# A norm cut into feature blocks and token columns, with three products fed in step

## The chip, the cores and the metric

The kernel runs on one core of one Trainium2 chip. The metric is the device time of one execution in microseconds, the median of several runs. Engines are named as the profile names them: PE (TensorE, with PEld for its weight loads), DVE (VectorE), ACT (ScalarE), POOL (GpSimd), SP (the queue that issues most reads).

## What is computed: the reference

Two layers over 512 latent and 256 context tokens of 1024 features:

```python
for l in range(DEPTH):                                   # 2
    mod_x = split(silu(c) @ ada_w[l] + ada_b[l], 6)      # shift, scale, gate of the mixer; the same of the MLP
    mod_c = split(silu(c_ctx) @ ada_w[l] + ada_b[l], 6)
    hx = rmsnorm(x, norm1_w[l]) * (1 + mod_x[1]) + mod_x[0]
    hc = rmsnorm(ctx, norm1_w[l]) * (1 + mod_c[1]) + mod_c[0]
    mix_x, mix_c = token_mixing(hx, hc, w_in[l], ...)    # z = h @ w_in; four head groups
    x = x + mod_x[2] * (mix_x @ w_out[l])
    h2 = rmsnorm(x, norm2_w[l]) * (1 + mod_x[4]) + mod_x[3]
    x = x + mod_x[5] * (square(relu(h2 @ mlp_w1[l])) @ mlp_w2[l])
    # ctx likewise with mod_c, but not in the last layer
return rmsnorm(x, final_norm_w)
```

The four head groups are a gated DeltaNet (GDN), windowed attention, a spatial-gating MLP and an mLSTM. Each takes its own columns of `w_in`.

## The kernel before

Tokens lie along the free dimension, features on the 128 partitions: `X` is eight tiles `x` of 128 features by 768 tokens, the context in columns 0 to 255, the latents in 256 to 767 (`ALL` names both pieces, `LAT` the second). The last layer's `w_out` and MLP run on the latents only.

Every large product is done in three matmuls per feature tile and column piece: weights and activations are each split into a rounded part and a remainder (`whi`, `wlo`; `hhi`, `hlo` for the modulated norm, `mhi` for the mixers' output, `fhi` for the MLP's hidden units), and `hhi*whi + hlo*whi + hhi*wlo` is summed in PSUM. ScalarE makes the rounded part, VectorE the remainder. `wload` reads 512 KB of weights by SP (`wst`) and splits them.

A norm goes in four steps. `sumsq` squares each feature tile on ScalarE and adds the squares on VectorE; after the eighth tile two matmuls per piece with a matrix of ones (`nrm`) give the sum over features in every partition. `modulated` turns it into 1/rms (`rstd`, two activations per piece), makes the scale `sc` and then, per feature tile and piece, `hy` = x * sc * rstd on VectorE, `hhi` on ScalarE and `hlo` on VectorE. `gemm_pair` then runs two products tile by tile, so that TensorE takes each h tile as it comes.

The modulation vectors are the product of `ada_w` (1024 by 6144) with the two conditioning vectors (`scT`). At the start, layer 0 needs the first 2048 columns: 16 reads of 512 KB (`adw`, 128 rows by 1024 columns each) feed matmuls of 32 stationary columns in four column groups (`adaps`); `ada_end` copies the sums (`adas`) and transposes them (`adat`) into `mod`. The other columns come later, between other work, in steps of VectorE (`adacc`).

At the start the x and ctx rows (`xs`) are read by ScalarE's queue, squared there and transposed by TensorE (`xps`) into `X`. The gates' product (32 columns: GDN's and mLSTM's gates) and GDN's first key product (`o_k0`) are run as the pair; the value product v0 and four more of GDN follow by `gemm`. The gates are transposed (`gatesT`) and worked on by VectorE in small steps (`ysp`, `gtmp`), and each product of GDN gets a five-tap convolution there (`kq`, `vf`). The order of instructions on each engine is that of the program as a scheduler lays it out, and each engine takes its own in that order.

There are four places at which a norm is made from x and a first product waits for it: the start, the middle of layer 0 (before `mlp_w1`), the passage to layer 1, the middle of layer 1.

## Time and profile before

| | us |
|---|---|
| median of 3 runs | 1973.33 |
| lowest and highest | 1965.30, 1974.22 |
| the profiled execution | 1960.3 |
| its span | 1958.5 |

The mean granted clock of TensorE over the span was 0.979 of the full one. The profiled execution lies 0.7% below the median; sums are made against it, and the difference is carried to the median. The page gives shares of busy time and groups of like instructions; the number ahead of an arrow is idle time of the engine before the row, with what ended it. Busy matmul rows overlap their neighbours, so the pace of the stream is read from the distance of two starts.

### The profile page before, as it was taken

The numbers are of one execution on the slowest core, as the hardware profiler recorded it, in microseconds if no ns is written. First come the engines' busy times: TensorE is split into PE (matmuls) and PEld (weight loads), VectorE is DVE, ScalarE is ACT, GpSimd is POOL, SyncE is SP. The second block draws the span as 40 slices with busy tenths as digits, with TensorE's granted clock in tenths as the row PEclk, the third lists the DMA queues.
The fourth block names the chain that finished last, engine by engine and source line by source line (L and its number), as shares of the span: only waits on it lengthen the run. The fifth ranks groups of instructions, "written<-read, shape, count | busy, mean of one in ns | idle before, by whom it ended". The sixth has DMA issues, their size and how long they took to land.

```text
span 1958.5 us, 33935 instructions
## 1 busy us (share of the span) xinstructions
PE 1881.4 (96%) x14107; PEld 1539.8 (79%) x14107; DVE 1196.3 (61%) x2210; ACT 754.2 (39%) x1528; POOL 101.1 (5%) x163
## 2 busy tenths in 40 slices
PE   6999999999899999999999999999999999999998
PEld 3877778778777888888888878677777778888887
DVE  3878875666659566435535349788777754444443
ACT  4652234455424312312213236534355543333242
POOL 0021210000000000000000000212100000000001
PEclk8999989999799999999999999999999999999999
DMA  9220001111364345335423222201011323333332
GB/s 324 80 52 24 23 13 44 57 55 44 120 203 128 109 140 147 94 116 151 129 84 122 81 62 54 63 23 34 23 44 33 102 76 103 97 97 97 97 97 76
DMA packets 225634, 172.28 MB, mean 88 GB/s; under 512 B 19042, under 2 KB 207816, under 8 KB 225480
## 3 DMA queue, kind: packets, MB, share of 16 engines
q1 hardware_dynamic: 219104, 153.38, 26.5%
q10 hardware_dynamic: 4680, 10.70, 1.5%
q0 software_dynamic: 1696, 6.03, 0.9%
q8 instruction: 110, 1.80, 0.4%
q14 instruction: 44, 0.36, 0.1%
HBM read 162.75 MB, written 7.34 MB: 87 GB/s over the span
## 4 chain that ended last, share of the span: by engine, by line
PE 82%; DVE 10%; ACT 4%; DMA 3%; issue 1%; POOL 0%; DVEq 0%; ACTq 0%; SPq 0%; POOLq 0%
PE mm L179 63%; PE mmt L179 2%; PE num L179 1%; PE ops L179 1%; DVE kq L188 1%; DMA wst<-w_in 1%; PE pv L179 1%; DVE wlo L185 1%; PE yt L179 1%; DVE Y L185 1%; PE adaps L179 1%; PE pT L1340 1%; PE t L179 1%; PE Eps L179 1%; PE yps L179 1%
## 5 line engine op out<-in xcount | busy, mean ns | idle before, releaser
L182 ACT ACTIVATE whi<-wst 128x512 fp32r<-128x512 f32 (+1 forms) x388 | 241.7, 627 | 682.2 <-PE mm L179 623.5
L179 PE MATMUL mm<-hhi,whi 128*128 128x512 f32 (+3 forms) x1344 | 477.8, 361 | 12.8 <-ACT hhi L182 11.4
L179 PE MATMUL mm<-hlo,whi 128*128 128x512 f32 (+3 forms) x1344 | 479.4, 357 | 1.5 <-DVE hlo L188 1.3
L179 PE MATMUL mm<-hhi,wlo 128*128 128x512 f32 (+3 forms) x1344 | 475.3, 356 | 0.1
L185 DVE TENSOR_TENSOR wlo<-wst,whi 128x512 fp32r<-128x512 f32 (+1 forms) x388 | 265.1, 687 | 313.3 <-ACT whi L182 309.4
L179 PEld LDWEIGHTS mm<-hhi,whi 128*128 128x128 f32 (+1 forms) x1344 | 251.9, 188 | 55.4 <-ACT hhi L182 14.9
L179 PEld LDWEIGHTS mm<-hlo,whi 128*128 128x128 f32 (+1 forms) x1344 | 253.1, 188 | 39.9 <-DVE hlo L188 3.6
L179 PEld LDWEIGHTS mm<-hhi,wlo 128*128 128x128 f32 (+1 forms) x1344 | 252.2, 188 | 39.0 <-issue 2.8
L179 PE MATMUL mm<-fhi,whi 128*128 128x512 f32 (+1 forms) x784 | 276.0, 352 | 0.0
L179 PE MATMUL mm<-flo,whi 128*128 128x512 f32 (+1 forms) x784 | 276.0, 352 | 0.0
L179 PE MATMUL mm<-fhi,wlo 128*128 128x512 f32 (+1 forms) x784 | 274.6, 350 | 0.0
L188 DVE SCALAR_TENSOR_TENSOR x<-mm,mod,x 128x256 f32<-128x256 f32 (+1 forms) x122 | 79.7, 653 | 142.4 <-PE mm L179 142.3
L179 PEld LDWEIGHTS mm<-fhi,whi 128*128 128x128 f32 x784 | 148.4, 189 | 21.7 <-ACT whi L182 0.8
L179 PEld LDWEIGHTS mm<-fhi,wlo 128*128 128x128 f32 x784 | 148.1, 189 | 19.7
L179 PEld LDWEIGHTS mm<-flo,whi 128*128 128x128 f32 x784 | 148.4, 189 | 19.2
L188 DVE SCALAR_TENSOR_TENSOR adacc<-adw,scT,adacc 128x1024 f32<-128x1024 f32 x84 | 105.8, 1281 | 28.3 <-DMA adw<-ada_w 28.2
L185 DVE TENSOR_TENSOR flo<-r,fhi 128x768 fp32r<-128x768 f32 (+1 forms) x64 | 52.6, 824 | 39.2 <-ACT fhi L182 39.1
L182 ACT ACTIVATE fhi<-r 128x768 fp32r<-128x768 f32 (+1 forms) x64 | 47.2, 740 | 66.8 <-DVE r L185 66.8
L179 PE MATMUL mm<-mlo,whi 128*128 128x512 f32 (+1 forms) x192 | 71.0, 370 | 1.3 <-DVE mlo L185 1.3
L179 PE MATMUL mm<-mhi,whi 128*128 128x512 f32 (+1 forms) x192 | 70.6, 368 | 0.4 <-ACT mhi L182 0.4
L179 PE MATMUL mm<-mhi,wlo 128*128 128x512 f32 (+1 forms) x192 | 70.0, 365 | 0.0
L182 ACT ACTIVATE r<-mm 128x256 f32<-128x256 f32 (+1 forms) x96 | 49.1, 514 | 31.5 <-PE mm L179 31.5
(404 smaller groups left out, 2712.3 us busy)
## 6 DMA issues: line engine op xcount, KB each, us to landing
wst<-mlp_w SPq DMA_DIRECT2D x128, 512.0 KB, 4.0
adw<-ada_w SPq DMA_DIRECT2D x96, 512.0 KB, 4.3
wst<-w_in SPq DMA_DIRECT2D x44, 512.0 KB, 3.7
wst<-w_out SPq DMA_DIRECT2D x64, 128.0 KB, 3.1
xd<-x ACTq DMA_DIRECT2D x8, 384.0 KB, 3.5
x<-xd POOLq DMA_DIRECT2D x8, 384.0 KB, 5.2
xs<-x ACTq DMA_DIRECT2D x4, 512.0 KB, 6.9
wst<-w_in SPq DMA_DIRECT2D x8, 256.0 KB, 3.4
```

Of the source, the lines that this page charges most:

```text
L179: T.matmul(o, lhsT=l, rhs=r, start=start, stop=stop)
L182: S.activation(out=o, in_=i, func=f, **kw)
L185: (eng or V).tensor_tensor(out=o, in0=a, in1=b, op=op)
L188: V.scalar_tensor_tensor(out=o, in0=a, scalar=s, in1=b, op0=op0, op1=op1)
L1340: T.transpose(o[:, 256 * i + 128 * g:256 * i + 128 * g + 128], Ps[g][:, 128 * (i0 + i):128 * (i0 + i) + 128], ident)
```

## The change

At the start, the modulation is made in four blocks of 256 features. Block c reads the shift's and the scale's columns of these features in four reads of 512 KB (128 rows by 4 by 256); four column groups of TensorE hold the partial sums of four row blocks each, and `csum`, a new constant, adds them in `adat`. `sc` is made per block. `block` makes one h tile (latents first, then context), and after each tile the gates, k0 and v0 products take their matmuls, three per product and piece. The latents' rows are read before the context's; a part of the constants is read earlier, the casts of others are written behind the products. The `adw` buffers, five, are four.

In the three later norms, the last two output tiles (6 and 7) of the product ahead are run column piece by column piece: latents, then context, or in the last layer two halves of 256 (`last_pair`). The first piece's norm sum, rstd and h stand among the second piece's matmuls. `gemm_first` then runs three products (gates, k0, v0, or three tiles of `mlp_w1`) on the first piece, and the second piece's h is made while it does. The steps of the later modulation sums are spread differently; those that layer 0 still has are all done before its last pair.

```diff
...
+LATF = ((256, 512), (0, 256))
...
     def sumsq(k, acc, segs, pl):
...
+        for i, (c0, cn) in segs:
+            x = X[k][:, c0:c0 + cn]
+            if k == 0:
+                sq = pl.tile([128, (512, 256)[i]], F32, tag="sqa%d" % i, name="sqa", bufs=1)[:, 0:cn]
+                acc[c0] = [sq]
+            else:
+                sq = pl.tile([128, NT], F32, tag="tc", name="sq", bufs=2)[:, 0:cn]
+            act_(sq, x, AF.Square)
+            if k == 7:
+                acc[c0].append(sq)
+            elif k:
+                tt(acc[c0][0], acc[c0][0], sq, ADD)
+    def norm_sum(acc, seg):
+        c0, cn = seg
+        o = ps("nrm")
+        for i, sq in enumerate(acc[c0]):
+            mm(o[:, 0:cn], ones, sq, i == 0, i == 1)
         return o
...
+    def modulation(l, which, ks=slice(0, 8)):
         base = 24 * which
         r0 = (R_N1, R_N2)[which]
         sc = per.tile([128, 8, 2], F32, tag="sc", name="sc")
...
         res = []
...
+        def scales(ks):
+            V.tensor_scalar(out=sc[:, ks], in0=mod[l][:, base + 8:base + 16, :][:, ks], scalar1=1.0, scalar2=None, op0=ADD)
+            tt(sc[:, ks], sc[:, ks], bc(prm[l][:, r0:r0 + 8][:, ks], 2, 2), MUL)
+        def rstd(seg, o, pl, bufs):
+            r = pl.tile([128, GAP + 4], F32, tag="tb", name="rstd", bufs=bufs)[:, 0:seg[1]]
+            act_(r, o[:, 0:seg[1]], AF.Ln, scale=1.0 / D, bias=eps)
+            act_(r, r, AF.Exp, scale=-0.5)
+            return r
+        def block(k, seg, r, pl):
+            c0, cn = seg
+            m = 1 if c0 == 0 else 0
+            s_ = slice(c0, c0 + cn)
+            if len(res) <= k:
+                res.append((hpool.tile([128, NT], F32R, tag="hi", name="hhi"),
+                            hpool.tile([128, NT], F32R, tag="lo", name="hlo")))
+            hi, lo = res[k]
+            y = pl.tile([128, GAP + 4], F32, tag="ta", name="hy", bufs=2)[:, 0:cn]
+            sh = mod[l][:, base + k, m:m + 1]
+            stt(y, X[k][:, s_], sc[:, k, m:m + 1], r, MUL, MUL)
+            act_(hi[:, s_], y, AF.Identity, bias=sh)
+            stt(lo[:, s_], y, sh, hi[:, s_].bitcast(F32), ADD, SUB)
+        def modulated(seg, o, pl, bufs):
+            r = rstd(seg, o, pl, bufs)
+            for k in range(8):
+                block(k, seg, r, pl)
+            return res
+        modulated.scales, modulated.rstd, modulated.block, modulated.res = scales, rstd, block, res
+        if ks:
+            scales(ks)
+        return modulated
...
-    for p in range(NP):
-        xs = ld.tile([128, D], F32, tag="xs", name="xs", bufs=6)
+    prow0 = ld.tile([128, 128], F32, tag="prow", name="prow", bufs=1)
+    for p in (2, 3, 4, 5, 0, 1):
+        if p == 0:
+            nc.scalar.dma_start(out=cst[:, 128:], in_=t["consts"][:, 128:NPERM])
+        xs = ld.tile([128, D], F32, tag="xs", name="xs", bufs=5)
...
-    ao = [ada_sum(0, 0, ld, go1("adaps")), ada_sum(0, 1, ld, gi("adaps"))]
-    params(0, ld.tile([128, 128], F32, tag="prow", name="prow", bufs=1))
-    for n in range(2):
-        ada_end(0, n, ld, ao[n])
+    params(0, prow0)
...
+    def gemm_step(w3, acts, seg, n, outs):
+        c0, cn = seg
         for k in range(8):
             ahi, alo = acts[k]
...
+            for o, n_, w_ in zip(outs, n, w3):
                 whi, wlo = w_[k // 4]
...
+                for pi, (w, a) in enumerate(((whi, ahi), (whi, alo), (wlo, ahi))):
+                    mm(o[0:n_, 0:cn], w[:, k % 4, 0:n_], a[:, c0:c0 + cn],
+                       start=(k == 0 and pi == 0), stop=(k == 7 and pi == 2))
+    def gemm_first(w3, acts, segs, n, between):
+        x = gs("mm3")
+        outs = []
+        for i, seg in enumerate(segs):
+            if i:
+                between()
+            outs.append([ps("mm"), ps("mm"), x[:, i]])
+            gemm_step(w3, acts, seg, n, outs[i])
+        return [[(outs[i][j], seg) for i, seg in enumerate(segs)] for j in range(3)]
+    def last_pair(w2, acts, l, g, segs, acc, pl, mk):
+        for i, seg in enumerate(segs):
+            for n in (6, 7):
+                o = gemm(None, acts, (seg,), w2=w2[n - 6])
+                if i and n == 6:
+                    o_n = norm_sum(acc, segs[0])
+                if i and n == 7:
+                    h_ = mk(segs[0], o_n, pl, 1)
+                residual(o, l, n, g, (seg,))
+                sumsq(n, acc, ((i, seg),), pl)
+        return h_
...
+    def ada_block(c, o):
+        for n in range(2):
+            for kh in range(2):
+                st = ld.tile([128, 4, 256], F32, tag="adw", name="adw", bufs=4)
+                nc.sync.dma_start(out=st, in_=t["ada_w"][0, 512 * kh:512 * kh + 512, 1024 * n + 256 * c:1024 * n + 256 * c + 256]
+                                  .rearrange("(k p) n -> p k n", p=128))
+                for k in range(4):
+                    mm(o[32 * k:32 * k + 32, 256 * n:256 * n + 256], scT[:, 4 * kh + k], st[:, k], n == kh == 0, n == kh == 1)
+        sb = ld.tile([128, 512], F32, tag="adas", name="adas", bufs=1)
+        act_(sb, o, AF.Copy)
+        o = go1("adat")
+        for i in range(4):
+            mm(o[:, 2 * i:2 * i + 2], sb[:, 128 * i:128 * i + 128], cc("csum"), i == 0, i == 3)
+        tt(mod[0][:, 0:16].rearrange("p (n f) m -> p n f m", n=2)[:, :, 2 * c:2 * c + 2, :],
+           o[:, 0:8].rearrange("p (n j m) -> p n j m", n=2, j=2),
+           bc(prm[0][:, R_ADA:R_ADA + 16].rearrange("p (n f) -> p n f", n=2)[:, :, 2 * c:2 * c + 2], 3, 2), ADD)
+    mk = modulation(0, 0, None)
+    r0 = {seg: mk.rstd(seg, nrm[bank(seg[0])], tp, 2) for seg in LATF}
+    ada_block(0, gi("ada"))
+    win = t["w_in"][0]
+    wset[:] = [(wsp, "whi", "wlo")] * 2 + [(ld, "bhi", "blo")] * 2
+    w3 = [wload([win[:, C_AB:C_AB + 16], win[:, C_IF:C_IF + 16]], own=ld), wload([win[:, C_GK:C_GK + 128]]), wload([win[:, C_GV:C_GV + 128]])]
+    o3 = [{bank(c0): ps("mm") for c0, cn in LATF} for _ in range(2)]
+    o = gs("mm3")
+    o3.append({0: o[:, 0], 1: o[:, 1]})
+    for c in range(4):
+        if c:
+            ada_block(c, gi("ada"))
+        mk.scales(slice(2 * c, 2 * c + 2))
+        for k in (2 * c, 2 * c + 1):
+            for seg in LATF:
+                mk.block(k, seg, r0[seg], tp)
+            hi, lo = mk.res[k]
+            for i, n in enumerate((32, 128, 128)):
+                whi, wlo = w3[i][k // 4]
+                for c0, cn in LATF:
+                    for pi, (w, a) in enumerate(((whi, hi), (whi, lo), (wlo, hi))):
+                        mm(o3[i][bank(c0)][0:n, 0:cn], w[:, k % 4, 0:n], a[:, c0:c0 + cn], k == pi == 0, k == 7 and pi == 2)
+    h = mk.res
...
-        ahead = [wload([win[:, C_AB:C_AB + 16], win[:, C_IF:C_IF + 16]]), wload([win[:, C_GK:C_GK + 128]])]
-        h = modulated(l, 0, ALL, nrm, tp)
-        del nrm
+        if l == 0:
+            first = o3
+        else:
+            w3 = [wload([win[:, C_AB:C_AB + 16], win[:, C_IF:C_IF + 16]], own=gd)]
+            w3 += [wload([win[:, c:c + 128]]) for c in (C_GK, C_GV)]
+            first = gemm_first(w3, h, LATF, (32, 128, 128), lambda: mk(LATF[1], nrm[0], tp, 2))
+            first = [{bank(seg[0]): o for o, seg in x} for x in first]
...
-            o = gemm(None, h, segs, w2=ready.pop(i)) if i else o_k0
-            if i < 5:
+            o = first[i + 1] if i < 2 else gemm(None, h, segs, w2=ready.pop(i))
+            if 0 < i < 5:
...
-        acc = []
+        acc = {}
         sums = ada_sums(todo, adp)
-        for n in range(8):
+        steps = HALVES if last else LATF
+        for n in range(6):
             o = gemm([t["w_out"][l][:, 128 * n:128 * n + 128]], mh, osegs, order=MIXK, w2=w_next.pop() if w_next else None)
             residual(o, l, n, 16, osegs)
-            nrm = sumsq(n, acc, osegs, tp)
-            for _ in range((2, 1, 1, 1, 1, 1, 1, 0)[n]):
+            sumsq(n, acc, tuple(enumerate(steps)), tp)
+            for _ in range((2, 1, 1, 1, 1, 2)[n]):
                 next(sums, None)
             if n == 3 and todo:
                 ada(*todo.pop(1), adp)
+        mk = modulation(l, 1)
+        h2 = last_pair([wload([t["w_out"][l][:, 128 * n:128 * n + 128]], MIXK) for n in (6, 7)], mh, l, 16, steps, acc, tp, mk)
         dbg(f"xa{l}", X[1][:, oc0:])
-        w2 = [wload([t["mlp_w1"][l][:, 128 * f:128 * f + 128]]) for f in range(2)]
-        h2 = modulated(l, 1, osegs, nrm, tp)
-        first = gemm_pair(w2, h2, osegs, (128, 128))
-        acc = []
+        w3 = [wload([t["mlp_w1"][l][:, 128 * f:128 * f + 128]]) for f in range(3)]
+        first = gemm_first(w3, h2, steps, (128,) * 3, lambda: mk(steps[1], norm_sum(acc, steps[1]), tp, 1))
+        acc = [] if last else {}
         for fb in range(4):
             hid = []
             for f in range(8):
-                if fb == 0 and f < 2:
+                if fb == 0 and f < 3:
                     o = first[f]
                 else:
                     o = gemm([t["mlp_w1"][l][:, 1024 * fb + 128 * f:1024 * fb + 128 * f + 128]], h2, osegs)
+                    o = [(o[bank(c0)], (c0, cn)) for c0, cn in osegs]
                 r = tp.tile([128, NT], F32, tag="tc", name="r")
-                for c0, cn in osegs:
-                    act_(r[:, c0:c0 + cn], o[bank(c0)][:, 0:cn], AF.Relu)
+                for x, (c0, cn) in o:
+                    act_(r[:, c0:c0 + cn], x[:, 0:cn], AF.Relu)
                 tt(r[:, ow], r[:, ow], r[:, ow], MUL)
...
-                next(sums, None)
-            tail = last and fb == 3
-            for n in range(6 if tail else 8):
+                for _ in range(1 if fb else (0, 2)[f > 3]):
+                    next(sums, None)
+            for n in range(6 if fb == 3 else 8):
                 o = gemm([t["mlp_w2"][l][1024 * fb:1024 * fb + 1024, 128 * n:128 * n + 128]], hid, osegs)
                 residual(o, l, n, 40, osegs)
-                if tail:
+                if fb == 3 and last:
                     finish(n, acc, tp, *LAT[0])
                 elif fb == 3:
-                    nrm = sumsq(n, acc, osegs, tp)
+                    sumsq(n, acc, tuple(enumerate(LATF)), tp)
                 next(sums, None)
-            if tail:
-                w2 = [wload([t["mlp_w2"][l][3072:4096, 128 * n:128 * n + 128]]) for n in (6, 7)]
+            if fb < 3:
+                continue
+            w2 = [wload([t["mlp_w2"][l][3072:4096, 128 * n:128 * n + 128]]) for n in (6, 7)]
+            if not last:
+                for _ in sums:
+                    pass
+                mk = modulation(l + 1, 0)
+                h = last_pair(w2, hid, l, 40, LATF, acc, tp, mk)
+                nrm = {0: norm_sum(acc, LATF[1])}
...
```

SP's queue at the start, before (`adw` the modulation's weights, `wst` those of `w_in`):

```order
L320 DMA adw<-ada_w 128x1024 x5
L488 DMA wst<-w_in 128x8x16
L320 DMA adw<-ada_w 128x1024 x11
L488 DMA wst<-w_in 128x8x16
L488 DMA wst<-w_in 128x8x128 x7
```

SP's queue at the start, after:

```order
L575 DMA adw<-ada_w 128x4x256 x4
L487 DMA wst<-w_in 128x8x16 x2
L487 DMA wst<-w_in 128x8x128
L575 DMA adw<-ada_w 128x4x256 x4
L487 DMA wst<-w_in 128x8x128
L575 DMA adw<-ada_w 128x4x256 x5
L487 DMA wst<-w_in 128x8x128 x2
L575 DMA adw<-ada_w 128x4x256 x3
```

All sixteen modulation reads stood ahead of k0's weights (the first of 128 columns); now eight stand ahead of v0's (the second of 128 columns), and eight behind.

PE at the start, before: the end of the modulation and the first product.

```order
L179 MATMUL adaps<-adw,scT 32x256 x4
L421 MATMUL prmT<-cst,prow 128x107
L179 MATMUL adaps<-adw,scT 32x256 x8
L179 MATMUL adat<-cst,adas 128x8 x2
L179 MATMUL mm<-hhi,whi 32x256
```

PE at the start, after, between the fourth and the fifth feature tile (`ada` holds block 2's and 3's partial sums, `wnhi` the gates' weights, `mm_360` is v0):

```order
L181 MATMUL mm_360<-hhi,wlo 128x256
L181 MATMUL ada<-adw,scT 32x256 x7
L181 MATMUL adat<-cst,adas 128x2 x4
L181 MATMUL ada<-adw,scT 32x256 x8
L181 MATMUL mm<-hhi,wnhi 32x512
L181 MATMUL mm<-hhi,whi 128x512
```

The whole modulation stood ahead of the first product; its third block now ends among the products.

PE at the passage to layer 1, before:

```order
L179 MATMUL mm<-fhi,wlo 128x512
L179 MATMUL nrm<-sq,ones 128x256
L179 MATMUL nrm<-sq,ones 128x512
L179 MATMUL nrm<-sq,ones 128x256
L179 MATMUL nrm<-sq,ones 128x512
L179 MATMUL mm<-hhi,whi 32x256
```

PE at the passage, after: the latents' norm sum (`sqa` the sum of seven squares, `sq` the eighth).

```order
L181 MATMUL mm<-fhi,wlo 128x256
L181 MATMUL nrm<-sqa,ones 128x512
L181 MATMUL nrm<-sq,ones 128x512
L181 MATMUL mm<-fhi,whi 128x256
```

PE at the passage, after, 24 matmuls later: the context's norm sum.

```order
L181 MATMUL mm<-fhi,wlo 128x256
L181 MATMUL nrm<-sqa,ones 128x256
L181 MATMUL nrm<-sq,ones 128x256
L181 MATMUL mm<-hhi,wnhi 32x512
```

The latents' norm sum has moved ahead of the last 24 matmuls of the product before it, the context's stands right ahead of the first product from h.

## Rows read from the trace of the kernel before

**Rows 1.** The page, shares of the engines and the dearest group from `hhi`.
```profile
PE 1881.4 (96%) x14107; PEld 1539.8 (79%) x14107; DVE 1196.3 (61%) x2210; ACT 754.2 (39%) x1528; POOL 101.1 (5%) x163
...
L179 PE MATMUL mm<-hhi,whi 128*128 128x512 f32 (+3 forms) x1344 | 477.8, 361 | 12.8 <-ACT hhi L182 11.4
```

**Rows 2.** Timeline of the start, all engines: start us, length us, instruction, idle before.
```profile
29.72 1.19 PE L403 MATMUL xps<-cst,xs 128*128 128x128 f32 x8 [2.20 <-DMA xs<-x]
...
36.10 0.62 ACT L182 ACTIVATE rstd<-rstd 128x512 f32<-128x512 f32 x1
...
39.15 0.38 ACT L182 ACTIVATE adas<-adaps 128x256 f32<-128x256 f32 x1 [2.44 <-PE adaps L179]
...
42.80 1.15 ACT L182 ACTIVATE whi<-wst 128x512 fp32r<-128x512 f32 x2 [1.04 <-DVE sc L251]
...
43.02 1.54 DVE L188 SCALAR_TENSOR_TENSOR hy<-x,sc,rstd 128x256 f32<-128x256 f32 x3
...
44.41 0.42 PE L179 MATMUL mm<-hhi,whi 128*32 128x256 f32 x1 [4.21 <-ACT hhi L182]
```

**Rows 3.** The page, DMA issues: count, KB each, median us to landing.
```profile
wst<-w_in SPq DMA_DIRECT2D x44, 512.0 KB, 3.7
```

**Rows 4.** View of the tile `adw` from 0 to 45 us.
```profile
DMA to landing us min/median/max: 4.0/6.0/9.1
```

**Rows 5.** Timeline of TensorE at the middle of layer 0, columns as in rows 2.
```profile
601.78 0.39 PE L179 MATMUL mm<-mhi,wlo 128*128 128x512 f32 x1
602.01 0.28 PE L179 MATMUL mm<-mhi,whi 128*128 128x256 f32 x1
602.12 0.28 PE L179 MATMUL mm<-mlo,whi 128*128 128x256 f32 x1
...
606.20 1.46 PE L179 MATMUL nrm<-sq,ones 128*128 128x256 f32 x4
608.27 1.56 PE L179 MATMUL nrm<-sq,ones 128*128 128x256 f32 x4 [0.62 <-ACT sq L182]
611.67 0.38 PE L179 MATMUL mm<-hhi,whi 128*128 128x256 f32 x1 [1.84 <-ACT hhi L182]
```

**Rows 6.** Chain of waits from 44 to 66 us: start us, us, what.
```profile
45.02 19.59 PE mm L179 x95
```

**Rows 7.** Busy us of PE, PEld, DVE, ACT, POOL by stretch, clock, DMA share, GB/s.
```profile
44.00:55.00 11.00, 10.40 (x44) 7.41 (x45) 11.00 (x22) 5.45 (x10) 0.20 (x2) 0.68 0.82 283
65.00:90.00 25.00, 25.00 (x146) 21.98 (x146) 24.22 (x46) 14.50 (x23) 0.62 (x12) 1.00 0.31 85
90.00:115.00 25.00, 24.55 (x145) 20.57 (x143) 17.99 (x37) 17.26 (x31) 0.52 (x4) 1.00 0.14 32
```

**Rows 8.** Timeline of VectorE at the middle of layer 0, columns as in rows 2.
```profile
607.81 2.47 DVE L188 SCALAR_TENSOR_TENSOR adacc<-adw,scT,adacc 128x1024 f32<-128x1024 f32 x2
610.20 0.87 DVE L188 SCALAR_TENSOR_TENSOR hy<-x,sc,rstd 128x256 f32<-128x256 f32 x2
611.25 0.75 DVE L188 SCALAR_TENSOR_TENSOR hy<-x,sc,rstd 128x512 f32<-128x512 f32 x1 [0.18 <-ACT rstd L182]
```

**Rows 9.** Timeline of TensorE at the passage to layer 1.
```profile
1162.34 1.56 PE L179 MATMUL nrm<-sq,ones 128*128 128x256 f32 x4 [0.49 <-ACT sq L182]
1166.10 0.31 PE L179 MATMUL mm<-hhi,whi 128*32 128x256 f32 x1 [2.21 <-ACT hhi L182]
```

**Rows 10.** Timeline of TensorE at the middle of layer 1.
```profile
1592.12 1.12 PE L179 MATMUL nrm<-sq,ones 128*128 128x512 f32 x2 [0.70 <-ACT sq L182]
1596.22 0.96 PE L179 MATMUL mm<-hhi,whi 128*128 128x512 f32 x3 [2.98 <-ACT hhi L182]
```

**Rows 11.** The same by stretch in layer 1, columns as in rows 7.
```profile
1165.00:1170.00 5.00, 3.23 (x12) 1.98 (x13) 4.93 (x9) 3.79 (x8) 0.52 (x3) 0.72 0.39 105
1210.00:1245.00 35.00, 34.30 (x228) 25.44 (x227) 27.26 (x57) 28.34 (x53) 8.01 (x16) 1.00 0.27 67
1595.00:1600.00 5.00, 3.78 (x11) 2.80 (x12) 4.74 (x8) 2.77 (x4) 0.00 (x0) 0.72 0.05 14
```

106 lines of the change are left out of this document (33 added, 73 removed).

## The prediction

> **What bounds the kernel now.** I read the shares of the engines first, then the waits of the dearest lines, then four stretches of the timeline. TensorE is busy 96% of the span and VectorE 61% [rows 1]. So in the long stretches nothing is to be had but TensorE's own work, which the change leaves alone: it issues 131 more TensorE instructions of 12931, most of them because 512 columns are cut into two times 256. What is left is in the places where the stream of products breaks. The group of all products from `hhi` sums its idle time before to 12.8 us, of which 11.4 us end with ScalarE writing `hhi` [rows 1]: a new norm, from which the first h is made. There are four such places: the start, the middle of layer 0, the passage to layer 1, the middle of layer 1. I reckon against the profiled execution (1960.3 us, span 1958.5) and carry the difference to the median of 1973.33.
>
> **The start: when the first product begins.** Now the last x rows land at 29.7, the rstd's last piece ends at 36.72, but h waits for the second modulation block: its copy `adas` is at 39.15, then VectorE does seven casts and the scales, and `hy` starts at 43.02, 1.39 before the first product at 44.41 [rows 2]. After, only the first 256 features (2 MB of the 8) are needed, the casts come later, and the ctx rows are asked for earlier. I estimate the last of them 2.7 us earlier (it is asked for at much the same time, but SP's reads have stopped by then, so it lands in some 4, near the 3.7 of [rows 3], rather than in 6 and more [rows 4]), thus rstd at 34.0. By rstd alone the first product would then be at 34.0 + 1.4 = 35.4. But on ScalarE the split of v0's weights now stands ahead of `hhi` (1.15 us, as in the row of 42.80 [rows 2]), and v0's read stands in SP's queue behind the wait for the gate weights' split. I place its issue at 32.4, an estimate from the steps ahead of it on VectorE, the landing 3.7 later [rows 3], the split and `hhi` behind it: first product 37.9. Bounds: 35.4, if the weights come early, and 40, if that read takes 6.0 as in the loaded start [rows 4]. So the first product gains about 6.5.
>
> **The start: what lies between.** A 512-column matmul takes 0.23 of the stream and a 256-column one 0.12 [rows 5], so a product (24 of each) takes 24 x 0.35 = 8.3 and a feature tile in three products 3.1. Before, the pair ran 44.4 to 64.6 [rows 6]. From 44 to 55 the granted clock was .68 in the mean, half the full one at first [rows 7], which costs 10.6 x .32 = 3.4; the rest, 16.8, is two products. v0 behind it ends at about 73. After: 37.9 + 4 x 3.1 + 3.4 (the same cold clock, since TensorE again idles before) = 53.7 for the first four tiles. Then comes what the order shows: the last 7 modulation matmuls of block 2 stand behind tile 3 and ahead of tile 4. From there it goes copy, `adat`, scale, `hy`, `hhi`: 0.4 + 0.6 + 0.5 + 0.5 + 1.4 = 3.4 by the steps of [rows 2], which nothing on TensorE covers but 16 of its own small matmuls. Block 3 has the same after tile 5, since its buffers (four) come free only when TensorE has read block 2: 3.6. So 53.7 + 3.4 + 6.2 + 3.6 + 6.2 = 73.1, and with a little cold clock again after the waits 74.3, where before stood 73.4: **+0.9**. Bounds: no wait at all gives 67.3 (-6.1); waits of 6.0 each [rows 4] and a clock that falls after both (1.7 each, as priced below) give 82.7 (+9.3).
>
> On top: gates and k0 were out at 64.6 [rows 6] while v0 still ran; now all three come out together at 74.3, so VectorE's gate and convolution chains start 9.7 later. From 65 to 90 VectorE is busy 24.22 of 25, from 90 to 115 17.99 of 25 [rows 7]. There are 7.8 us of slack to take the 9.7: **+2** (0 if the next stretch hides it, +9.7 if none does, because the chain of gates and not the sum of work counts; I take the sum, since the convolutions and splits between are freely mixed there). The start together +2.9, from -6 to +11.
>
> One rule speaks against products in step. The Trainium skill, TensorEngine Tiling (Array Packing), "Key Properties", says that changing the tiling mode drains TensorE; gates take 32 columns and the others 128, and the three products change width 41 times, where the pair did 35 times. The pair's 16.8 above against 2 x 8.3 = 16.6 [rows 6] leaves 0.2 for 35 changes; by the row the six more cost 0.03, by the rule some drain each, and no sum here holds it.
>
> **The three later norms.** From the last product to the first one from h pass 606.20 to 611.67 in the middle of layer 0 [rows 5], 5.5 us: norm sums, rstd, `hy`, `hhi`; the two others have the same steps. After the change 48 matmuls of 256 columns, 48 x 0.12 = 5.8, stand between the first segment's last residual and its first h, so that chain is just covered; the second segment's lies beside 72 matmuls of the first. What stays in each is the second segment's norm sum, which TensorE meets before its square is there: a residual and a square, some 1.3 at their 256 columns, less what stands before, say 0.8 (the waits for a square now are 0.49 to 0.70 [rows 5, 9, 10]).
>
> Middle of layer 0: idle 0.62 and 1.84 [rows 5]. Then VectorE makes a tile's `hy` and `hlo` in 2 x (0.43 + 0.70) = 2.3 [rows 8] (two 256-column pieces overlap in 0.87), TensorE reads it in 6 x 0.35 = 2.1: over eight tiles some 1.8 lost. Sum 4.3; in three products a tile of the first segment takes 9 x 0.23 = 2.1 and needs 1.4 of VectorE, so that loss goes too. Against it the 0.8, and VectorE has two `adacc` steps (2.47 [rows 8]) ahead of `hy` as now, which may cost a part of the cover: **-3** (-4 to -1).
>
> Passage: idle 0.49 and 2.21 [rows 9], the 1.8 as above, and a clock of .72 in 1165 to 1170 [rows 11]: 5 x .28 = 1.4, 1.7 with what follows. 6.2 less 0.8: **-5.4**; no `adacc` stands in the way, since the sums are drained before. But gates and k0 come out 8.3 later relative to the first h, as at the start, so 8.3 - 5.4 = 2.9 later in time. From 1210 to 1245 VectorE is busy 27.26 of 35 [rows 11], 7.7 of slack: taken as +1 (0 to +3). Net -4.4, bounds -6.5 to -1.
>
> Middle of layer 1 (latents alone): idle 0.70 and 2.98 [rows 10], and clock .72 in 1595 to 1600 [rows 11], 1.7 again: 5.4. The 0.8 stays, and 512 columns become 2 x 256 in 48 + 72 matmuls at some 0.01 each, +1: **-3.5** (-4.5 to -2).
>
> The edits that add nothing: splitting the squares by segment (ScalarE is idle there), the modulation sums moved to other places of the MLP (VectorE is idle there, the waits are for DMA), x rows in another order. In the GDN stretch of layer 1 the order of small steps moves as well; the trace can't price it, so 0, +-3.
>
> **Sum:** 2.9 - 3 - 4.4 - 3.5 = -8.0, on the profiled execution 1952.3, on the median 1965.3.
>
> **The rivals.** (a) *The start pays in full.* Blocks 2 and 3 are there in time and TensorE doesn't wait: -6.1 instead of +0.9, and gates come 2.7 later (67.3) rather than 9.7, which the slack takes. Sum -6.1 - 3 - 4.4 - 3.5 = -17.0: 1956. For it speaks that DMA is nearly done by 30 and free thereafter; against it stands the place of block 2's last matmuls in TensorE's order and the four buffers.
>
> (b) *Slower: VectorE's gate chain is the path.* If the slack of [rows 7, 11] can't be used, because GDN waits for the last step of the gates and not for the convolutions, gates 9.7 late cost 9.7 in layer 0 and 2.9 in layer 1 (instead of -4.4): 9.7 - 3 + 2.9 - 3.5 = +6.1, 1979; with the two waits at 6.0 and a fallen clock, gates 18 late, +14.3, 1988. It makes the kernel slower from gates 3.6 late without slack, and beyond 0.5% from 13.5 late, gates at 78. For it: VectorE is 97% busy from 65 to 90. Against: 28% idle behind.
>
> (c) *The norms don't pay.* h of the first segment still waits, because `hy` stands behind other work of VectorE, so the cover ends before h is there. Then about 2 of each 4 to 5 remains, the sum is 2.9 - 1 - 1 - 1.5 = -0.6: 1973.
>
> **How the numbers follow.** My forecast 0.52, (a) 0.25, (b) 0.13, (c) 0.10. About 0.5% (9.9 us) is what a measurement of this kernel can tell from no change. The forecast's own range is -16 to 0, of which 0.3 lies beyond -9.9; (a) lies there almost wholly; of (b) most lies beyond +9.9 only if the waits are long as well. Faster 0.16 + 0.23 = 0.39, slower 0.11, the rest same. The range takes in (a), (c) and the nearer end of (b), and the bounds of the start: 1950 to 1983.
>
> **What would show it.** First product at 37.9 (35.4 to 40). TensorE idle behind tiles 3 and 5 for about 3.5 each, ended by `hhi`, with a fallen clock after; if these waits are missing, (a). Gates at 74 and VectorE full to 105; if GDN's first chains in layer 0 start over 6 later than before, (b). The group of products from `hhi` falls from 11.4 of waits to about 9, nearly all of it at the start; if 2 us stay at each norm, (c). The clock at 1.00 in all three later passages. The forecast is wrong above all if VectorE's late start isn't absorbed, or if the reads of blocks 2 and 3 are much later or earlier than I place them.

## The result and the profile after

| | before | after |
|---|---|---|
| median, first comparison | 1970.33 (4 runs) | 1990.93 (4 runs) |
| ratio, 95% interval | | 1.0104 [1.0076, 1.0132] |
| median, second comparison | 1968.39 (31 runs) | 1985.30 (10 runs) |
| ratio, 95% interval | | 1.0086 [1.0062, 1.0109] |
| profiled execution | 1960.3 | 1986.3 |
| its span, mean granted clock | 1958.5, 0.979 | 1984.2, 0.973 |

(The first comparison's runs of before are the three of the section on the time before, and one more.) The change makes the kernel about 1% slower: 17 to 21 us, where 8 us less were forecast. The page of after, engine shares and two groups (busy us, mean ns, then idle time before, with what ended it); they answer [rows 1]:

```profile
PE 1894.7 (95%) x14255; PEld 1558.6 (79%) x14255; DVE 1199.9 (60%) x2254; ACT 759.5 (38%) x1567; POOL 98.7 (5%) x163
...
L181 PE MATMUL mm<-hhi,whi 128*128 128x512 f32 (+1 forms) x1336 | 475.1, 357 | 5.6 <-ACT hhi L184 3.7 <-ACT vt L184 0.9 <-ACT P L184 0.4
...
L181 PE MATMUL mm<-hhi,wnhi 128*32 128x512 f32 (+1 forms) x32 | 11.7, 370 | 12.9 <-ACT wnhi L184 9.5 <-ACT hhi L184 3.4
```

The waits for h did shrink: 11.4 before, now 3.7 and 3.4. But a wait of 9.5 for `wnhi`, the split gate weights, stands beside them. TensorE's idle time (span less busy) is 89.5, where it was 77.1: 12.4 more, half of the 25.7 between the two spans. The other half is busy time, 13.3 more; it comes from a lower clock, and from small matmuls that I come to.

**The passage.** Timeline of TensorE in after from 1160 to 1192 (start, length, instruction, idle before it), which answers [rows 9]; then ScalarE and VectorE there:

```profile
1172.75 1.02 PE L181 MATMUL nrm<-sqa,ones 128*128 128x512 f32 x2
...
1179.24 0.70 PE L181 MATMUL nrm<-sq,ones 128*128 128x256 f32 x2 [1.31 <-ACT sq L184]
1189.39 0.64 PE L181 MATMUL mm<-hhi,wnhi 128*32 128x512 f32 x1 [9.45 <-ACT wnhi L184]
```

```profile
1176.83 1.39 ACT L184 ACTIVATE hhi<-hy,mod 128x512 fp32r<-128x512 f32 x2 [0.82 <-DVE hy L190]
...
1189.03 0.51 ACT L184 ACTIVATE wnhi<-wst 128x128 fp32r<-128x128 f32 x2 [0.60 <-DVE hlo L190]
```

```profile
1187.59 1.80 DVE L190 SCALAR_TENSOR_TENSOR hlo<-hy,mod,hhi 128x512 fp32r<-128x512 f32 x3
```

The first `hhi` are written from 1176.83 on, in good time for the chain that was forecast. As far as h goes, the product could begin soon behind them; it begins at 1189.39, because ScalarE splits the gate weights only behind all eight latent tiles. The split waits for VectorE's last `hlo`, which reads `hy`. Their read is asked for at 1143.85, 45 us earlier. What the split lacks is room: its tiles are in `gd`, a pool opened over the MLP's pools, in which `hy` still lies. By stretch (busy of PE, PEld, DVE, ACT, POOL, granted clock, DMA share, GB/s):

```profile
1180.00:1190.00 10.00, 0.61 (x2) 0.18 (x2) 9.71 (x20) 6.62 (x14) 1.10 (x4) 0.63 0.00 0
1190.00:1200.00 10.00, 10.00 (x40) 7.03 (x39) 6.38 (x16) 3.31 (x8) 0.59 (x4) 0.86 0.38 105
```

TensorE does nothing for 9.45 us, and then has 0.86 of its clock in the mean of ten us, a mixture of its lower level (half speed) and the full one.

**The start**, TensorE, against [rows 2] and [rows 6]; then the row of VectorE that the wait of 1.68 rests on:

```profile
40.13 0.64 PE L181 MATMUL mm<-hhi,wnhi 128*32 128x512 f32 x1
...
47.54 0.42 PE L181 MATMUL mm<-hlo,wnhi 128*32 128x512 f32 x1 [1.68 <-DVE hlo L190]
...
57.04 1.06 PE L181 MATMUL ada<-adw,scT 128*32 128x256 f32 x14
58.87 1.05 PE L181 MATMUL adat<-cst,adas 128*128 128x2 f32 x8 [0.77 <-ACT adas L184]
59.86 1.07 PE L181 MATMUL ada<-adw,scT 128*32 128x256 f32 x16
62.13 0.42 PE L181 MATMUL mm<-hhi,wnhi 128*32 128x512 f32 x1 [1.20 <-ACT hhi L184]
...
68.55 1.07 PE L181 MATMUL ada<-adw,scT 128*32 128x256 f32 x16
70.40 1.05 PE L181 MATMUL adat<-cst,adas 128*128 128x2 f32 x8 [0.78 <-ACT adas L184]
73.65 0.63 PE L181 MATMUL mm<-hhi,wnhi 128*32 128x512 f32 x1 [2.20 <-ACT hhi L184]
...
81.36 0.56 PE L728 MATMUL gatesT<-cst,ta 32*128 32x32 f32 x6
```

```profile
45.66 0.23 DVE L618 CAST gmask_r<-cst 128x128 fp32r<-128x128 f32 x1 [3.07 <-DMA cst<-consts]
```

The pauses before tiles 4 and 6 are there (57.04 to 62.13 and 68.55 to 73.65), 5.1 us each. A third wait, before tile 1, comes from VectorE: casts of constants whose read lands at 45.6 stand in its order ahead of the next `hlo`.

**The middles.** Layer 0, TensorE, then VectorE (compare [rows 5, 8]); layer 1, TensorE (compare [rows 10]):

```profile
628.29 0.96 PE L181 MATMUL mm<-hhi,whi 128*128 128x512 f32 x3 [1.47 <-ACT hhi L184]
629.09 0.59 PE L181 MATMUL nrm<-sqa,ones 128*128 128x256 f32 x2
```

```profile
624.35 2.48 DVE L190 SCALAR_TENSOR_TENSOR adacc<-adw,scT,adacc 128x1024 f32<-128x1024 f32 x2
626.74 1.41 DVE L190 SCALAR_TENSOR_TENSOR hy<-x,sc,rstd 128x512 f32<-128x512 f32 x2
```

```profile
1615.13 0.59 PE L181 MATMUL nrm<-sqa,ones 128*128 128x256 f32 x2
1615.56 0.59 PE L181 MATMUL nrm<-sq,ones 128*128 128x256 f32 x2
...
1627.75 0.59 PE L181 MATMUL nrm<-sqa,ones 128*128 128x256 f32 x2
1628.18 0.59 PE L181 MATMUL nrm<-sq,ones 128*128 128x256 f32 x2
1631.04 0.62 PE L181 MATMUL mm<-hhi,whi 128*128 128x256 f32 x3 [2.26 <-ACT hhi L184]
```

In layer 1 no wait is left at the first half's norm, but the second half's norm sum stands behind the first half's products, and its rstd and h are made with TensorE idle: 2.26 stay, where before waited 0.70 and 2.98. In layer 0 the two `adacc` stand ahead of `hy`, and 1.47 stay. These two are the 3.7 of the page.

Where the time went, as the start of the same instruction in the profiled executions, after less before:

| step | time in before | after less before |
|---|---|---|
| first product from h | 44.4 | -4.3 |
| gates out, layer 0 | 64.5 | +16.8 |
| GDN's first chain, layer 0 | 138.5 | +10.8 |
| end of GDN, layer 0 | 294.3 | +10.2 |
| `w_out`, layer 0 | 524.3 | +18.8 |
| end of `mlp_w1`, layer 0 | 1092.1 | +15.3 |
| gates out, layer 1 | 1185.5 | +30.7 |
| GDN's first chain, layer 1 | 1247.1 | +26.5 |
| `w_out`, layer 1 | 1544.3 | +28.6 |
| end of `mlp_w1`, layer 1 | 1902.5 | +25.6 |

So in this pair of profiles the start costs 10.8, the passage 11.2 (15.3 to 26.5); the middles give 3.5 and 3.0 back. The 8.0 and 2.1 more in the mixers, which the change leaves alone, are read below, and so is what the other profiles give for each stretch.

### The profile page after: what moved, and what is told of

It is laid out like the page before. It is cut to its first block, busy times and chain, and to the rows that moved or that the text cites. A ratio compares the mean times of both kernels' runs of the same rounds, so it can differ in the third digit from the quotient of the medians.

```text
span 1984.2 us, 34313 instructions
## 1 busy us (share of the span) xinstructions
PE 1894.7 (95%) x14255; PEld 1558.6 (79%) x14255; DVE 1199.9 (60%) x2254; ACT 759.5 (38%) x1567; POOL 98.7 (5%) x163
## 4 chain that ended last, share of the span: by engine, by line
PE 83%; DVE 9%; ACT 3%; DMA 3%; issue 1%; POOL 0%; DVEq 0%; ACTq 0%; SPq 0%; POOLq 0%
PE mm L181 63%; PE mmt L181 3%; PE num L181 2%; PE ops L181 1%; PE pv L181 1%; DVE Y L187 1%; PE t L181 1%; PE Eps L181 1%; PE yt L181 1%; PE pT L1432 1%; PE yps L181 1%; DVE wlo L187 1%; PE adaps L181 1%; DMA xs<-x 1%; DMA adw<-ada_w 1%
## 5 line engine op out<-in xcount | busy, mean ns | idle before, releaser
L184 ACT ACTIVATE whi<-wst 128x512 fp32r<-128x512 f32 x384 | 239.7, 630 | 654.4 <-PE mm L181 581.0
L181 PE MATMUL mm<-hhi,whi 128*128 128x512 f32 (+1 forms) x1336 | 475.1, 357 | 5.6 <-ACT hhi L184 3.7
L181 PE MATMUL mm<-hlo,whi 128*128 128x512 f32 (+1 forms) x1336 | 471.7, 353 | 0.0
L181 PE MATMUL mm<-hhi,wlo 128*128 128x512 f32 (+1 forms) x1336 | 469.3, 353 | 1.5 <-DVE wlo L187 1.3
L187 DVE TENSOR_TENSOR wlo<-wst,whi 128x512 fp32r<-128x512 f32 x384 | 263.3, 690 | 326.5 <-ACT whi L184 324.3
L181 PEld LDWEIGHTS mm<-hhi,whi 128*128 128x128 f32 x1336 | 254.4, 191 | 45.4 <-ACT hhi L184 4.3
L181 PEld LDWEIGHTS mm<-hhi,wlo 128*128 128x128 f32 x1336 | 253.4, 190 | 38.2 <-DVE wlo L187 3.9
L181 PEld LDWEIGHTS mm<-hlo,whi 128*128 128x128 f32 x1336 | 254.5, 190 | 32.6 <-issue 1.3
L181 PE MATMUL mm<-mhi,whi 128*128 128x512 f32 (+1 forms) x208 | 73.6, 354 | 0.4 <-ACT mhi L184 0.4
L184 ACT ACTIVATE r<-mm 128x256 f32<-128x256 f32 (+1 forms) x99 | 49.5, 505 | 30.7 <-PE mm L181 29.2
```

What stands on the lines that cost most here:

```text
L181: T.matmul(o, lhsT=l, rhs=r, start=start, stop=stop)
L184: S.activation(out=o, in_=i, func=f, **kw)
L187: (eng or V).tensor_tensor(out=o, in0=a, in1=b, op=op)
```

## The experiments

Times within one kernel differ by its clock: 84 executions of before lie between 1958.2 us at a mean granted clock of 0.983 and 1985.3 at 0.965, on a line of 15 us per 0.01. So the table has, beside the medians, the median difference to before when each execution is moved along that line to 0.975 (before: 1969.1). That column takes away clock which a kernel may itself have lost, so it is read beside the ratio, not in its place. The idle time of TensorE is of the one profiled execution, as a difference to the 77.1 of before.

| kernel | median | ratio to before, 95% | idle | at clock 0.975 |
|---|---|---|---|---|
| after, 4 runs | 1990.93 | 1.0104 [1.0076, 1.0132] | +12.4 | +12.4 |
| after_again, 10 | 1985.30 | 1.0086 [1.0062, 1.0109] | +11.4 | +12.2 |
| e1_start_only | 1979.13 | 1.0040 [1.0012, 1.0068] | +4.7 | +4.5 |
| e2_norms_only | 1977.25 | 1.0044 [1.0010, 1.0078] | +8.8 | +5.9 |
| e3_wn | 1976.00 | 1.0040 [1.0011, 1.0070] | -0.8 | +3.0 |
| e4_triple, 4 | 1993.38 | 1.0121 [1.0072, 1.0169] | +12.0 | +14.3 |
| e6_ahead | 1974.40 | 1.0015 [0.9992, 1.0038] | +5.6 | +5.1 |
| e7_norms_pair, 7 | 1957.93 | 0.9920 [0.9896, 0.9944] | -4.9 | -8.2 |
| e8_all_pair | 1967.19 | 0.9962 [0.9932, 0.9992] | -2.8 | -2.4 |
| e9_delay | 1983.59 | 1.0056 [1.0034, 1.0078] | +15.7 | +8.7 |
| e10_triple0 | 1973.43 | 1.0024 [0.9996, 1.0052] | +2.2 | +2.7 |
| e11_wn_ahead | 1970.40 | 1.0001 [0.9978, 1.0025] | -4.6 | 0.0 |
| e12_norms_wn | 1963.00 | 0.9975 [0.9946, 1.0003] | -3.9 | -4.2 |

Rows without a number have 10 runs.

**The two halves apart.** e1_start_only keeps the new start and takes the later norms of before; e2_norms_only the other way.

```diff
 e1
-            first = gemm_first(w3, h, LATF, (32, 128, 128), ...)
+            h = modulated_old(l, 0, ALL, nrm, tp)
+            first = gemm_pair(ahead, h, ALL, (32, 128)) + [None]
 e2
-    for c in range(4):
-        if c:
-            ada_block(c, gi("ada"))
...
+    ao = [ada_sum(0, 0, ld, go1("adaps")), ada_sum(0, 1, ld, gi("adaps"))]
```

> The start of the changed kernel, with the three later norms as they were before. Theory (the start is half of the loss: gates come out 17 us late, and the gated DeltaNet starts 11 us late because of it): the first product at about 40, gates at about 81, the DeltaNet 9 to 11 us later than before, layer 1 then keeps that shift and adds nothing; the time is 11 to 19 us above that of the kernel before (19 if the clock's falls in layer 0 come out as unluckily as in the changed kernel). Rival (the later norms are to blame for all): within 4 us of the kernel before.

> The start of the kernel before, with the three later norms of the changed kernel. Theory (the passage to layer 1 costs 13 us since TensorE waits 9.5 us for the gates' weights, the two others gain 3 each): 5 to 9 us above the kernel before, with the gates of layer 1 about 14 us later than before relative to the end of layer 0. Rival (the passage is slow only because everything ahead came late): 5 to 11 us below the kernel before.

Either half alone is slower, by 0.4%. The ledger of e1 has GDN's first chain at +14.6 in layer 0, that of e2 at +2.4; in e2 the passage costs 10.3 (7.6 to 17.9). Both losses of after are there, each with its half. The medians are 9.2 and 7.3 above before; that of e1 lies below the 11 to 19 that were expected.

**The passage: another room for the gate weights' split.** e3_wn is after with the split's tiles in a pool of their own, opened ahead of the MLP's pools on the other side of SBUF. The order of the operations in the program's text stays.

```diff
-            w3 = [wload([win[:, C_AB:C_AB + 16], win[:, C_IF:C_IF + 16]], own=gd)]
+            w3 = [wload([win[:, C_AB:C_AB + 16], win[:, C_IF:C_IF + 16]], own=wnp)]
...
+            wnp = wn_.enter_context(tc.tile_pool(name="wnp", bufs=2, side="right"))
```

> The changed kernel, with the split weights of layer 1's gates in a small room of their own, which is free before the MLP's rooms are given back; v0's weights still lie in the later room. Theory (the 9.5 us wait at the passage is a wait for room: the gates' weights take the place of the temporaries in which the last norm is made): the wait goes, the first product of layer 1 comes 8 to 9.5 us earlier, the time falls by 8 to 13 us against the changed kernel, to about 1980. Rival (the wait for h would take its place, since VectorE makes h one tile after the other): a fall of at most 3 us.

All waits of TensorE over 0.7 us from 1150 to 1270 in e3 (total, times, longest); the same view of after from 1160 to 1270 begins with 9.5 for `wnhi`:

```profile
PE t L181 <- DVE Z L940: 2.0, 1, 2.0
PE mm L181 <- DVE wlo L187: 0.9, 1, 0.9
```

The wait is gone, and so is the low clock behind it:

```profile
1180.00:1190.00 10.00, 10.00 (x48) 7.66 (x47) 9.27 (x22) 5.96 (x12) 1.36 (x3) 1.00 0.21 54
```

ScalarE now splits the gate weights 30 us ahead of the first `hhi` (1170.40 here):

```profile
1140.66 0.51 ACT L184 ACTIVATE wnhi<-wst 128x128 fp32r<-128x128 f32 x2
```

From the end of `mlp_w1` to GDN's first chain in layer 1, e3 is 2.1 faster than before (8.9 to 6.8), where after is 11.2 slower. With that the cause at the passage is shown: the room, and not the data. The scheduler's order moved with it: in after the split stands behind all eight latent `hhi` on ScalarE, in e3 ahead of them. That the one follows from the other is argued: a split that waits for the last `hlo` can't stand ahead of the `hhi` from which that `hlo` is made. No run has the free room with the old place of the split.

**The start: the modulation's blocks one pair of tiles earlier.** e6_ahead is after with block c+1 written behind the first tile of block c, so that its small matmuls, copy and scale run while the second tile does.

```diff
-        if c:
-            ada_block(c, gi("ada"))
...
+            if k % 2 == 0 and c < 3:
+                ada_block(c + 1, gi("ada"))
```

> The changed kernel, with the modulation's block c+1 written between the two feature tiles of block c rather than behind them, so that its copy, transposition and scales run while products do. Theory (at the start TensorE waits 5 us ahead of tile 4 and 5 us ahead of tile 6 because of the place of the block, not of its reads, which have landed): these two waits fall to under 1 us each, the gates come 7 to 10 us earlier than in the changed kernel, at 71 to 74, and the time falls by 3 to 8 us. Rival (the reads are late): the waits stay over 3 us each, under 2 us in all.

The waits of TensorE in e6 from 40 to 110:

```profile
PE mm L181 <- DVE hlo L190: 1.9, 2, 1.3
...
PE adat L181 <- ACT adas L184: 0.7, 1, 0.7
```

No wait for `hhi` is left, yet the gates come out at 78.4, 13.8 later than before, and not at the 71 to 74 expected. The first product lies elsewhere in each execution, so the gates are better counted from it: 20.1 behind it in before, 41.2 in after, 35.8 in e6. The two waits (2.0 and 3.0) are what e6 wins; what remains is work. Busy time of the blocks' sums (`ada`) and of their transposing (`adat`) in after, between the first product and the gates:

```profile
40.00:82.00 42.00, 4.66 (x60) 0.93 0.55 188
...
40.00:82.00 42.00, 2.11 (x16) 0.93 0.55 188
```

6.8 us of TensorE's time lie there. In before this work ran ahead of the first product; between its first product and its gates there is none of it. A run below, e10, has the same three products and the old start: its gates are 29.1 behind the first product, 6.7 less than in e6, at nearly the same clock (0.94 and 0.95) and idle time (1.5 and 1.9). So the 21.1 that after loses between first product and gates are 9.0 for the third product, 6.7 for the blocks' matmuls and 5.4 for the waits.

**Both mends, and the old start with the new norms.** e11_wn_ahead is after with the edits of e3 and e6; e12_norms_wn is e2 with the edit of e3.

> The changed kernel with both mends: layer 1's gate weights in a room of their own, and block c+1 of the modulation written between the tiles of block c. If the two losses add up (15 us for the room, 3 to 16 for the blocks), 0 to 8 us below the kernel before; if they are one and the same, still some 3 to 6 us above it.

> The start of the kernel before, the later norms of the changed kernel with three products in step at the passage, and the gates' weights in a room of their own. It differs from the fastest so far (1957.9) only by the third product at the passage. If the third product costs 1 to 2 us by the gates' late end, it is 8 to 14 us below the kernel before; if the deferral itself is dear, within 6 us of it.

The two mends take away the whole loss: e11 equals before. e12 is 5.4 below it, less than the 8 to 14 expected. The two differ from one another in the start alone, and that is worth 4 to 7 us against the new start (at equal clock 0.0 and -4.2), near to the 4.4 by which GDN's first chain is later in e11. But the new start holds the third product too, and the blocks' matmuls are not these 4 us: in e11 the first three products are out 1.4 later than in before (74.9 to 73.6), since their 6.8 us and an earlier first product nearly cancel. The other 3.0 arise behind the gates; their cause was not isolated. In e12 the later norms give what they were made for: from the end of `mlp_w1` to GDN's chain 2.3 at the passage (-5.3 to -7.6), 2.1 in the middle of layer 0, 3.0 in that of layer 1.

**Three products in step, alone.** e4_triple is before with v0 fed in step with gates and k0 in both layers; e10_triple0 does it in layer 0 only.

```diff
-        o, o_k0 = gemm_pair(ahead, h, ALL, (32, 128))
+        first = gemm_pair(ahead, h, ALL, (32, 128, 128))
```

> The kernel before, with three products in step (gates, k0, v0) in place of two at the head of both layers, and nothing else. It defers the gates and k0 by one product (8.3 us) in each layer and leaves TensorE's work as it is. Theory (rival b of the prediction: VectorE's gate chain is on the path): the gated DeltaNet starts 5 to 8 us later in each layer, 10 to 16 us in all. The prediction's view (VectorE's slack takes it): 0 to 3 us in all.

> The kernel before with three products in step at the head of layer 0 alone; layer 1 keeps the pair. The gates come out 8 to 10 us later. If VectorE's slack takes what the prediction gave it, the gated DeltaNet starts 1 to 3 us later and the time is 0 to 4 us above; if the deferral itself is dear, as the 23 us of the kernel with three products in both layers let one think, 8 to 14 us.

e10 has the gates out 10.7 later and GDN's first chain 2.2 later: 8.5 are taken up. Of the 2.2, 1.8 are a later first product (46.2; with the old start it lies between 44.4 and 46.9). All profiles together show what it goes with: GDN's first chain is as late as the end of the first three products, also where the gates are later than that (here and in e4). In before they end at 73.6 and the chain begins at 138.5; in e2, e4, e7, e8, e9, e10 and e12 both have moved by the same, within 0.6. In the six profiles with the new start and three products in step (after, after_again, e1, e3, e6, e11) the chain is 2.9 to 4.0 later than that. In e4's layer 1 the gates lose 8.9 (10.9 to 19.8) and the chain 3.5 (10.9 to 14.4). That price, about 2 and 3, agrees with e10's 0.2% and with +2.7 at equal clock. The 1.2% of e4 do not follow from it: its profile has 3.5 us more idle time in GDN of layer 1, and for the rest a lower clock in both mixers. It is a result of four executions, and its size stays open.

**The old start, and pairs in place of three.** e7_norms_pair is e12 with only gates and k0 in step at the passage; e8_all_pair is e11 with pairs at the start and the passage.

```diff
-            w3 += [wload([win[:, c:c + 128]]) for c in (C_GK, C_GV)]
-            first = gemm_first(w3, h, LATF, (32, 128, 128), lambda: mk(LATF[1], nrm[0], tp, 2))
+            w3 += [wload([win[:, C_GK:C_GK + 128]])]
+            first = gemm_first(w3, h, LATF, (32, 128), lambda: mk(LATF[1], nrm[0], tp, 2))
```

> The start of the kernel before; the three later norms by columns, but at the passage to layer 1 two products in step (gates, k0) as before, v0 behind them, and the gates' weights in a room of their own. Theory (norms by columns gain 3 to 5 us each, if neither the weights' room nor the third product stands in the way): first product of layer 1 about 5 us earlier relative to the end of layer 0, 7 to 13 us below the kernel before. Rival (the gain is lost to the clock in the mixers that follow): within 4 us of the kernel before.

> As the last, and with the changed kernel's start too, but with two products in step there and block c+1 of the modulation written between the tiles of block c. Theory (the blocks pay at the start, if TensorE does not wait for them and the gates are not put off): first product at 40, gates at 60 to 64, 3 to 8 us below the one with the old start. Rival (the pieces of modulation between the products cost as much as the earlier first product gains): equal to it, within 3 us.

e7 is the fastest of all, 0.8% faster than before: later norms by columns, the split in a room of its own, the old start, pairs. Its passage takes 3.2 less than before's (2.3 to -0.9), e12's 2.3. The 0.9 between them is all that their traces show; the 5 us between their medians are more than that, and the two were run beside different sets of before. e8 says again that the blocks don't pay: it lies 9 us above e7 in the median and 5.8 at equal clock, where 3 to 8 below were expected. The first product is at 41.8, near the 40 expected, but the gates are at 74.1 and not at 60 to 64. Here TensorE waits 4.5 for the modulation's reads, since a pair consumes a block sooner:

```profile
PE ada L181 <- DMA adw<-ada_w: 4.5, 4, 2.1
```

**Is it the phase?** The mixers of after lost 10 us though the change leaves them alone; a rival was that a late start as such shifts them against the clock. e9_delay is before with a chain of VectorE steps, which change nothing, ahead of the first h.

```diff
+        if l == which == 0:
+            for _ in range(50):
+                V.tensor_scalar(out=sc, in0=sc, scalar1=1.0, scalar2=None, op0=MUL)
```

> The kernel before with a chain of 46 small steps on VectorE ahead of the first h, which put off everything behind by some 8 us and change nothing else. Theory (a late start costs what it is late, and the clock's falls later in the run scatter from execution to execution): all marks from the gates to the end 6 to 10 us later, the time 6 to 10 us above. Rival (where the start lies decides how the clock falls in the mixers): the shift of the last marks differs from that of the first by over 5 us in the median.

```profile
57.48 0.42 PE L179 MATMUL mm<-hhi,whi 128*32 128x256 f32 x1 [14.51 <-ACT hhi L182]
```

The first product is 13.1 later, GDN's chain 12.9 later, the median 10.9. A delay costs about what it is long, and no more. The marks of the one profile don't keep that distance: from `w_out` of layer 1 on they are 24 to 26 later, after a stretch in which TensorE lost 10 us to a low clock and before's profile none; the median says that this is the execution and not the delay. Here gates and first three products are late together, and nothing is taken up.

**Once more.** after_again is after unchanged, beside more runs of before.

> The changed kernel once more, beside the others and with more executions. Its time was the median of four, all with a low mean clock (0.967 to 0.973, where the kernel before has 0.965 to 0.983). If the loss is the two steps that the traces show, it stays 17 to 22 us above the kernel before; if half of it was the clock of four executions, 9 to 14 us.

The loss is confirmed at 0.9%, and at equal clock it is the same 12 us.

**All profiles together.** Each of the 14 profiles has the same stretches, some with the old form and some with the new one. Medians (lowest to highest), from the start of one instruction to that of another:

| stretch | old form | new form | new less old |
|---|---|---|---|
| start to GDN's first chain | 139.0 (138.3 to 140.8), 4 | 152.6 (149.3 to 153.6), 4 | +13.6 |
| end of `mlp_w1` to GDN's chain in layer 1 | 155.5 (155.0 to 155.6), 4 | 165.9 (165.4 to 166.5), 4 | +10.4 |
| the same with the free room | | 152.8 (152.7 to 152.9), 3 | -2.7 |
| `w_out` to the end of `mlp_w1`, layer 0 | 567.0 (566.6 to 569.6), 5 | 562.9 (562.3 to 565.8), 9 | -4.1 |
| the same, layer 1 | 356.4 (356.3 to 358.1), 5 | 355.1 (355.1 to 358.0), 9 | -1.3 |
| GDN's chain to `w_out`, layer 0 | 388.9 (382.9 to 393.5), 7 | 386.6 (383.1 to 393.8), 7 | -2.3 |
| the same, layer 1 | 302.1 (297.2 to 311.9), 5 | 303.7 (298.5 to 307.5), 9 | +1.6 |

The start leaves out e4, e6, e8, e9, e10 and e11, the passage e4, e7 and e8, whose forms lie between. The mixers' own operations are changed by no edit; their rows are parted by the start in layer 0 and by the norms in layer 1. The start, the passage and the two middles come to +18.6, which agrees with the measured loss of 17 to 21. In the mixers the old and the new kernels spread over much the same times.

## Why the prediction was wrong

- **First product at 37.9:** at 40.13, 4.3 earlier than before instead of 6.5, just outside the bound of 40. The six other profiles with this start have it between 39.1 and 42.7, five of them at 41.8 or later, so the forecast was some 4 early.
- **Tiles 0 to 3 until 53.7:** 57.0, of which 2.2 is the late start; the wait of 1.68 at tile 1 and 1.3 of the blocks' matmuls were not foreseen. That no more than 1.1 shows is luck: the cold clock, set at 3.4, cost 1.2 (0.51 of the full clock from 40.1 to 42.5, the lower level, then 1.00). I had put the later casts of constants down as a gain and not asked when their read lands, and VectorE takes them in its order, ahead of `hlo`.
- **Pauses of 3.4 and 3.6:** the place was right, the size was not: 5.1 each. Of these 2.0 and 3.0 are waits; the rest is the small matmuls. I named the latter only as cover ("16 of its own small matmuls"). The step of the start that failed is theirs: the sum held 0.6 for `adat` in each pause and nothing for the rest of the 6.8 us, and the first three products ended at 81.4 in place of 74.3, 7.8 later than before's 73.6 in place of 0.9. This is also why rival (a), the start in full, could not have come: without those waits e6 and e11 have the gates 36 behind their first product, where (a) had 29.4. (In both bounds of the start a slip keeps 1.2 of cold clock that belongs to the waits: by my own terms they are 66.1 and 81.5, not 67.3 and 82.7. And the counts of 131 and 12931 instructions stand in no view; the pages have 14107 and 14255 matmul records.)
- **No drain counted between widths:** the tiles of block 2 take 6.42 from 62.13 to 68.55, against 6.2 by columns alone; seven changes of width lie in them, and 37, not 41, in the three products. The rule that I weighed (the Trainium skill, TensorEngine Tiling (Array Packing), "Key Properties") gives no size, and this row leaves little for one.
- **7.8 of slack on VectorE:** after took up 6.0 (16.8 to 10.8), e10 8.5. With the true 16.8 my own step gives 9.0, measured 10.8. So rival (b), no slack, is refuted by e10, though its test (GDN over 6 later) came true. But the mechanism was put wrongly: GDN's chain goes with the end of the first three products and not with the gates, as e10 and e4 tell the two apart. My sum had both terms, +0.9 and +2; they measured +7.8 and +3.0.
- **Passage -4.4:** +11.2 in after. The step that failed is the one that lets layer 1's first product begin when its h is there ("no `adacc` stands in the way"): a wait for its weights was put at nothing, and it was 9.45. I looked for what stands ahead of h, and not for what stands ahead of the other operand. The split of the gate weights got tiles in a pool whose room was not yet free. No rival had it. With the room free the step measures -2.1 to -2.3 against before's profile (e3, e11, e12): right in sign, half in size.
- **Middle of layer 0, -3:** -3.5, with the `adacc` wait where I feared it. **Middle of layer 1, -3.5:** -3.0, but by luck. The second half's chain did not lie beside the first half's matmuls, as I had it, but behind them, and 2.26 of the wait stayed, the size that rival (c) gave, by another way than its own. TensorE's idle time in that stretch fell by 1.4 only (4.2 to 2.8); the rest is that before's profile lost 3.4 us there to a low clock and after's none. After_again lost 3.2, and is 0.1 shorter than before. Over all profiles the gain is 1.3. In the middles the wait for the square (0.8 each) did not appear; at the passage it was 1.31.
- **The clock at 1.00 in three later passages:** in the middle of layer 1 yes; at the passage 0.63 and 0.86.
- **GDN and the rest 0, ±3:** in the profiled pair +8.0 and +2.1. This is clock. Summed over short windows (busy time times one less the granted clock), the stretch from GDN's end to `w_out` in layer 0 lost 10.9 us to it in before and 21.6 in after. Of the difference 3.8 (9.53 x 0.40) lie in the ten us behind one wait of 1.46 at `Mt`, which both have (at 341.25 in before, 351.42 in after). These ten us in before, then in after (columns as above):

```profile
341.00:351.00 10.00, 9.65 (x78) 9.35 (x79) 9.65 (x20) 0.90 (x3) 0.00 (x0) 1.00 0.11 20
```

```profile
351.00:361.00 10.00, 9.53 (x47) 9.11 (x48) 7.43 (x17) 0.89 (x3) 0.00 (x0) 0.60 0.01 2
```

  And the same place, behind the same wait (1.45 at 354.43), in after_again, which is the same kernel as after:

```profile
354.00:364.00 10.00, 9.46 (x76) 9.15 (x77) 9.65 (x20) 0.90 (x3) 0.00 (x0) 1.00 0.09 20
```

  Its stretch lost 11.7, and its mixers of layer 0 are 2.7 shorter than before's. So the 8.0 belong to one execution and not to the change.

- **The base:** I summed against an execution with a clock of 0.979, where the median one of before has 0.975. Carrying the difference to the median, as I did, was right; but marks of single executions hold some 10 us of such scatter, in both directions.

In one line: the start cost 11 to 15 in the profiles in place of 3, the passage 10 to 11 in place of -4, and the middles gave 5.4 in place of 6.5. Shown by runs that undo them: the passage's room (e3), the start's pauses (e6), both together (e11); shown by comparing runs: that the blocks' matmuls take 6.7 between first product and gates (e6, e10), and that the mixers' loss in after's profile is scatter (after_again). Argued: that the place of the split on ScalarE follows from the room. Open: the 3 to 4 us by which GDN's chain is later than the first three products in the new start with three in step; e4's size; and whether after lowers the mean clock by itself (its 10 later executions have a median of 0.9725, before's 84 of 0.975).
